# Feed-forward block products summed in the accumulator: one bank grows p1, p6, p7, p4, another p5, p3

## The chip, the core and the metric

The kernel runs on one core of a Trainium2 chip. The metric is the device time of one execution in microseconds (us). The core has five instruction queues that matter here: TensorE (PE, matrix multiply; PEld is its weight load), VectorE (DVE), ScalarE (ACT), GpSimd (POOL) and SyncE (SP, which issues the DMAs). Each queue runs its instructions in the order in which they stand; they wait for each other by semaphores.

## The reference

One inference step of a one-layer encoder. 512 prompt frames and 8 x 16 sample frames make 640 tokens of width 2048. After two kinds of attention and an output projection comes a SwiGLU block with 5632 hidden columns, which takes the larger part of the time and is what the change touches:

```python
def merge_and_ffn(x, oa, ob, norm_grp_a, norm_grp_b, w_out, norm_ffn, w_gate, w_up, w_down):
    o = jnp.concatenate([rmsnorm(oa, norm_grp_a), rmsnorm(ob, norm_grp_b)], axis=-1)
    x = x + o @ w_out
    h = rmsnorm(x, norm_ffn)
    return x + (jax.nn.silu(h @ w_gate) * (h @ w_up)) @ w_down
```

## The kernel before

Everything is float32. A product of two float32 matrices is made of three fast matmuls: each operand is split in a rounded high half (made by ACT, L138) and the rest, the low half (made by DVE, L139), and `mm3` adds high x high, high x low and low x high in PSUM (L147, L148, L149).

In the feed-forward block the products are not taken plainly. Weights and activations are cut in 2 x 2 blocks, and seven products p1 to p7 of sums of blocks give the four result blocks c11, c12, c21, c22 (Winograd's form of Strassen's scheme), instead of eight. The generator `quartet` makes these seven products for one quartet of blocks: it loads the weight blocks b11, b12, b21, b22 by DMA, forms b12-b22 and s6 = b11-(b12-b22) on DVE (L826, L828), b22-s6 and b21-s6 on POOL (L830, L837), and `product` splits one weight operand (list "H" holds six tiles, so three products' halves exist at once) and issues the matmuls of one product: k blocks x 3, with 320 columns. After each product it yields the PSUM bank, and the caller adds that bank where it belongs (L847) or copies it (L886, L960). With u = p1+p6 the results are c11 = p1+p2, c12 = u+p5+p3, c22 = u+p7+p5, c21 = u+p7+p4.

- The loop over w_gate and w_up runs 44 quartets with k = 8: 24 matmuls a product. Activations h stay in SBUF as seven sets of halves (`hs`). Behind each w_gate quartet stand a norm factor, Silu and another factor (L909 to L911), behind each w_up quartet the product with the gate (L915) and the sums for the next stage on POOL (L919 to L922), which four DMAs write to DRAM (act_d).
- w_down runs 32 steps t (`step`), with k = 5 (t below 8 and from 24) or 6, so 15 or 18 matmuls a product. Each of the 8 column groups q is visited four times; its sums x and y stay in SBUF, and u = p1+p6 has a sum of its own over the four visits (tile `us`), which the last visit (t from 24) adds to c21, c22 and c12. Between steps one pair of activations leaves and another is fetched from act_d and split (L857 to L860).
- The last w_up quartet also fetches and splits the five pairs that step 0 needs (`free`, L871), product by product.
- Steps 30 and 31 are cut in an "early" part (p1, p6, p7, p5, p4: the second half of the tokens is finished first) and a "late" part (p2, p3), with the final norm between.

Weight tiles ("W") are six slots in turn: a load waits until the last reader of the slot's former tile is done. PSUM has two pairs of banks (`n.banks()`, named dn) and four single banks (`n.bank()`, named at). Before, a quartet took both pairs: x[:, 0] for p1, x[:, 1] for p5, y[:, 0] for p6, y[:, 1] for p3; p7, p2 and p4 had single banks. The order in each queue is set by the Tile framework's scheduler, not by the order of the source alone.

Of the kernel before, what the change touches and what calls it, by code (L numbers as in the profile page):

```python
# [7 lines left out]
AF = mybir.ActivationFunctionType  # L8
# [5 lines left out]
P = 128  # L14
# [35 lines left out]
class Net:  # L50
# [94 lines left out]
    def mm3(self, out, a, b, first, last):  # L145
        mm = self.nc.tensor.matmul
        mm(out, a[0], b[0], start=first, stop=False)  # L147
        mm(out, a[0], b[1], start=False, stop=False)  # L148
        mm(out, a[1], b[0], start=False, stop=last)  # L149
# [85 lines left out]
def build(nc, tc, io, pools):  # L235
# [557 lines left out]
    def quartet(k, load, lefts, before=None, after=None, part="all"):  # L793

        def product(src, which, bank):
            own = n.get("H"), n.get("H")
            hl = [r(sh(x, k, P)) for x in own]  # L800
            n.split(sh(src, k, P), *hl)
            if before:
                before(which)
            for j in range(k):
                n.mm3(bank, (hl[0][:, j], hl[1][:, j]), lefts[j][which][1], j == 0, j == k - 1)
            n.put("H", *own)
            if after:
                after(which)
            return bank

        def get(i):
            t = n.get("W")
            dma(out=sh(t, k, P), in_=load(i))
            return t

        w = slice(0, k * P)
        sub = ALU.subtract
        if part == "late":
            b21, b22 = get(2), get(3)
            for name, src, which in (("p2", b21, 4), ("p3", b22, 6)):  # L820
                yield name, product(src, which, n.bank()[:, :HT])
                n.put("W", src)
            return
        x, y = n.banks(), n.banks()
        b12, b22, b11 = get(1), get(3), get(0)
        nc.vector.tensor_tensor(b12[:, w], b12[:, w], b22[:, w], sub)  # L826
        s6 = n.get("W")
        nc.vector.tensor_tensor(s6[:, w], b11[:, w], b12[:, w], sub)  # L828
        yield "p1", product(b11, 0, x[:, 0])
        nc.gpsimd.tensor_tensor(b11[:, w], b22[:, w], s6[:, w], sub)  # L830
        yield "p6", product(s6, 1, y[:, 0])
        yield "p7", product(b12, 2, n.bank()[:, :HT])
        n.put("W", b12)
        b21 = get(2)
        if part == "all":
            yield "p2", product(b21, 4, n.bank()[:, :HT])
        nc.gpsimd.tensor_tensor(b21[:, w], b21[:, w], s6[:, w], sub)  # L837
        n.put("W", s6)
        yield "p5", product(b11, 3, x[:, 1])
        n.put("W", b11)  # L840
        yield "p4", product(b21, 5, n.bank()[:, :HT])
        n.put("W", b21)
        if part == "all":
            yield "p3", product(b22, 6, y[:, 1])
        n.put("W", b22)
# [31 lines left out]
    for i in range(NPAIR):  # L877
        for src in ("w_gate", "w_up"):
# [5 lines left out]
            for step, bank in quartet(8, load, hs, (lambda w: next(prep)) if start else None, free if end else None):  # L884
                if step == "p1":
                    nc.scalar.activation(c11, bank, AF.Identity)  # L886
                elif step == "p6":
                    add(c12, c11, bank)
                elif step == "p7":
                    add(c21, c12, bank)  # L890
                elif step == "p5":
                    add(c22, c21, bank)
                    add(c12, c12, bank)
                elif step == "p2":
                    add(c11, c11, bank)
                elif step == "p4":
                    add(c21, c21, bank)
                elif step == "p3":
                    add(c12, c12, bank)
# [37 lines left out]
    def step(t, part="all"):  # L937
        now = active(t)
        nxt = active(t + 1) if t + 1 < STEPS else []
        cnt, q, last = len(now), t % 8, t >= STEPS - 8  # L940
# [6 lines left out]
        if t < 8:  # L947
            x, y = n.get("S"), n.get("S")
            dma(out=x, in_=x2_d[q])
            dma(out=y, in_=x2_d[q + 8])  # L950
            sums.append((x, y, n.get("S") if q % 2 == 0 else sums[-1][2]))
        x, y, u = sums[q]
        c11, c21, c12, c22 = x[:, :HT], x[:, HT:], y[:, :HT], y[:, HT:]
        us = u[:, HT * (q % 2):HT * (q % 2) + HT]
        o = 2 * sum(len(active(i)) for i in range(q, t, 8))
        load = lambda z: io["w_down"][q + 8 * (z % 2), :, o + cnt * (z // 2):o + cnt * (z // 2) + cnt]
        for name, bank in quartet(cnt, load, [lefts[j] for j in now], None, after, part):
            if name == "p1":
                if t < 8:
                    nc.scalar.activation(us, bank, AF.Identity)  # L960
                else:
                    add(us, us, bank)
                add(c11, c11, bank)
            elif name == "p6":
                add(us, us, bank)
                if last:
                    for c in (c21, c22, c12):
                        add(c, c, us)
            elif name == "p7":
                add(c21, c21, bank)  # L970
                add(c22, c22, bank)
            elif name == "p5":
                add(c22, c22, bank)
                add(c12, c12, bank)
            elif name == "p2":
                add(c11, c11, bank)
            elif name == "p4":
                add(c21, c21, bank)
            elif name == "p3":
                add(c12, c12, bank)  # L980
# [147 lines left out]
```

## Time and profile before

| what | value |
|---|---|
| three timed runs, median | 2710.97 us (2708.78 to 2711.12) |
| the profiled execution: time, span | 2706.72 us, 2705.0 us |
| mean granted TensorE clock | 0.986 |
| PE, DVE, ACT, POOL busy | 97%, 71%, 40%, 29% of the span |
| w_gate and w_up | from about 1000 us to about 2095 us |
| w_down, steps 0 to 31 | from about 2095 us to about 2680 us |

The profile is of one execution. Its groups give the mean duration of like instructions, the timeline each instruction with the idle time before it and what ended it, and the table by windows the busy time and the number of instructions of each engine in a stretch. Matmuls overlap their neighbours, so in a stretch without waits the number of matmuls says more than the busy time.

### The profile page before, as it was taken

How to read it: one execution, taken by the hardware profiler on the slowest of the kernel's cores; microseconds unless marked ns; L12 is line 12 of the kernel's file. 1: busy time of each engine (PE TensorE's matmuls, PEld its weight loads, DVE VectorE, ACT ScalarE, POOL GpSimd, SP SyncE). 2: the span in 40 equal slices, each digit the busy share in tenths (PEclk: the TensorE clock that was granted, in tenths of full speed). 3: DMA queues.
4: the chain of work that ended last, by engine and by line, in shares of the span. 5: the costliest groups of instructions: out<-in, count | busy, mean ns of one | idle time of the engine just before them, and what ended most of it. 6: DMA issues, size and time to landing. Idle time of an engine off the chain costs nothing.

```text
span 2705.0 us, 44972 instructions
## 1 busy us (share of the span) xinstructions
PE 2629.3 (97%) x17629; PEld 2568.5 (95%) x17629; DVE 1928.6 (71%) x2956; ACT 1084.0 (40%) x1759; POOL 786.9 (29%) x564
## 2 busy tenths in 40 slices
PE   7999999999999999999999999999999999999986
PEld 7999999999899999999999999999999899999986
DVE  7565565665766777667767666676668888888897
ACT  4333343444633553333333333333334444444443
POOL 3000000000211123343333333433334534444453
PEclk9999999999999999999999999999999899999997
DMA  5222223333556443333333333333335644444344
GB/s 166 85 73 82 89 68 108 109 119 114 183 187 217 147 134 104 104 119 103 105 115 108 108 121 100 119 102 109 113 106 173 214 130 127 132 133 130 107 116 135
DMA packets 154147, 332.23 MB, mean 123 GB/s; under 512 B 18064, under 2 KB 69264, under 8 KB 153936
## 3 DMA queue, kind: packets, MB, share of 16 engines
q1 hardware_dynamic: 153936, 329.38, 38.8%
q8 instruction: 138, 2.26, 0.4%
q14 instruction: 73, 0.60, 0.1%
HBM read 274.38 MB, written 54.20 MB: 121 GB/s over the span
## 4 chain that ended last, share of the span: by engine, by line
PE 84%; DVE 8%; DMA 4%; issue 3%; ACT 2%; SPq 0%; DVEq 0%; POOL 0%; ACTq 0%
PE dn L147 18%; PE dn L149 17%; PE dn L148 17%; PE at L147 9%; PE at L149 9%; PE at L148 9%; DVE W L139 2%; PE at L254 1%; DVE S L847 1%; DMA S<-act_d 1%; DMA W<-w_down 1%; DVE S L139 1%; PE at L155 1%; PE at L154 1%; DVE S L1018 0%
## 5 line engine op out<-in xcount | busy, mean ns | idle before, releaser
L147 PE MATMUL dn<-S,W 128*128 128x320 f32 x3694 | 1165.9, 316 | 15.4 <-DVE S L847 9.6
L149 PE MATMUL dn<-S,W 128*128 128x320 f32 x3694 | 1152.1, 312 | 14.0 <-DVE W L139 13.8
L148 PE MATMUL dn<-S,W 128*128 128x320 f32 x3694 | 1150.3, 311 | 1.1 <-DVE S L139 1.1
L138 ACT ACTIVATE W<-W 128x1024 fp32r<-128x1024 f32 (+2 forms) x632 | 609.3, 965 | 1045.1 <-PE dn L148 518.0
L139 DVE TENSOR_TENSOR W<-W,W 128x1024 fp32r<-128x1024 f32 (+2 forms) x632 | 768.3, 1216 | 126.6 <-ACT W L138 122.3
L147 PEld LDWEIGHTS dn<-S,W 128*128 128x128 f32 x3694 | 700.6, 190 | 33.2 <-issue 16.9
L149 PEld LDWEIGHTS dn<-S,W 128*128 128x128 f32 x3694 | 700.3, 190 | 19.4 <-DVE W L139 18.9
L148 PEld LDWEIGHTS dn<-S,W 128*128 128x128 f32 x3694 | 701.1, 190 | 3.0 <-DVE S L139 1.3
L149 PE MATMUL at<-S,W 128*128 128x320 f32 x1594 | 494.4, 310 | 7.0 <-DVE W L139 6.6
L147 PE MATMUL at<-S,W 128*128 128x320 f32 x1594 | 493.5, 310 | 1.5 <-ACT W L138 1.5
L148 PE MATMUL at<-S,W 128*128 128x320 f32 x1594 | 493.0, 309 | 0.0
L830 POOL TENSOR_TENSOR W<-W,W 128x1024 f32<-128x1024 f32 (+2 forms) x76 | 162.5, 2138 | 588.0 <-DVE W L139 519.0
L149 PEld LDWEIGHTS at<-S,W 128*128 128x128 f32 x1594 | 299.5, 188 | 10.2 <-DVE W L139 10.2
L147 PEld LDWEIGHTS at<-S,W 128*128 128x128 f32 x1594 | 299.9, 188 | 1.7 <-ACT W L138 1.7
L148 PEld LDWEIGHTS at<-S,W 128*128 128x128 f32 x1594 | 299.6, 188 | 0.0
L847 DVE TENSOR_TENSOR S<-S,dn 128x320 f32<-128x320 f32 x358 | 164.2, 482 | 97.6 <-PE dn L149 97.6
L826 DVE TENSOR_TENSOR W<-W,W 128x1024 f32<-128x1024 f32 (+2 forms) x76 | 134.5, 1770 | 103.9 <-DMA W<-w_up 52.4
L837 POOL TENSOR_TENSOR W<-W,W 128x1024 f32<-128x1024 f32 (+2 forms) x76 | 165.5, 2178 | 111.9 <-DVE W L139 106.5
L847 DVE TENSOR_TENSOR S<-S,at 128x320 f32<-128x320 f32 x262 | 123.5, 481 | 70.1 <-PE at L149 70.0
L218 POOL TENSOR_TENSOR S<-S,S 128x640 f32<-128x640 f32 x40 | 75.7, 1893 | 155.5 <-ACT S L217 155.1
L828 DVE TENSOR_TENSOR W<-W,W 128x1024 f32<-128x1024 f32 (+2 forms) x76 | 82.9, 1091 | 30.7 <-DMA W<-w_gate 24.1
L139 DVE TENSOR_TENSOR S<-at,S 128x512 fp32r<-128x512 f32 (+2 forms) x109 | 64.1, 600 | 50.3 <-ACT S L138 49.9
(149 smaller groups left out, 2351.0 us busy)
## 6 DMA issues: line engine op xcount, KB each, us to landing
W<-w_gate SPq DMA_DIRECT2D x88, 512.0 KB
W<-w_up SPq DMA_DIRECT2D x88, 512.0 KB
W<-w_in SPq DMA_DIRECT2D x66, 512.0 KB
W<-w_down SPq DMA_DIRECT2D x64, 384.0 KB
W<-w_down SPq DMA_DIRECT2D x68, 320.0 KB
act_d<-S SPq DMA_DIRECT2D x66, 320.0 KB
half<-act_d SPq DMA_DIRECT2D x81, 160.0 KB
S<-act_d SPq DMA_DIRECT2D x80, 160.0 KB
```

The source lines that it names most:

```text
L138: self.nc.scalar.activation(hi, src, AF.Identity)
L139: self.nc.vector.tensor_tensor(lo, src, f(hi), ALU.subtract)
L147: mm(out, a[0], b[0], start=first, stop=False)
L148: mm(out, a[0], b[1], start=False, stop=False)
L149: mm(out, a[1], b[0], start=False, stop=last)
L154: mm(out, a, b[0], start=first, stop=False)
L218: (eng or nc.gpsimd).tensor_tensor(ssq, ssq, sq, ALU.add)
L826: nc.vector.tensor_tensor(b12[:, w], b12[:, w], b22[:, w], sub)
L828: nc.vector.tensor_tensor(s6[:, w], b11[:, w], b12[:, w], sub)
L830: nc.gpsimd.tensor_tensor(b11[:, w], b22[:, w], s6[:, w], sub)
L837: nc.gpsimd.tensor_tensor(b21[:, w], b21[:, w], s6[:, w], sub)
L847: add = lambda o, a, b: nc.vector.tensor_tensor(o, a, b, ALU.add)
```

## The change

p1, p6, p7 and p4 now go to one bank x of one pair, without clearing it in between (`first=False`; the new argument `more` of `mm3` only lifts the check that a group is closed): after p1 the bank holds p1, after p6 u, after p7 u+p7 and after p4 u+p7+p4. p5 and p3 go to the other bank y of the pair in the same way. Only p2 has a single bank. Each bank is read after each product and before the next product that adds to it. `us`, its tiles and its adds are gone. The order becomes p1, p2, p6, p5, p7, p3, p4; the first quartet ("lean") keeps p1, p6, p7, p2, p5, p4, p3, and the "early" parts run p1, p5, p6, p4, p7. The loads come in the order b11, b21, b12, b22. In w_gate and w_up four of the seven reads are now copies on ACT and three are adds on DVE (one copy and seven adds before); in w_down there are seven adds on DVE (9 and a copy for t below 8, 10 up to t = 23, 13 from t = 24).

```diff
-        mm(out, a[0], b[0], start=first, stop=False)
+        mm(out, a[0], b[0], start=first, stop=False, skip_group_check=more)
...
+        pair_of = n.banks()
+        x, y = pair_of[:, 0], pair_of[:, 1]
+        b11 = get(0)
+        def sums():
+            b12, b22, s6 = get(1), get(3), n.get("W")
+            minus(b12, b12, b22)
+            minus(s6, b11, b12)
+            return b12, b22, s6
...
+        b21 = get(2)
+        yield "p1", product(b11, 0, x)
...
+        yield "p2", product(b21, 4, alone())
+        b12, b22, s6 = sums()
+        yield "p6", product(s6, 1, x, False)
+        minus(b11, b22, s6, nc.gpsimd)
+        yield "p5", product(b11, 3, y)
+        n.put("W", b11)
+        minus(b21, b21, s6, nc.gpsimd)
+        n.put("W", s6)
+        yield "p7", product(b12, 2, x, False)
+        n.put("W", b12)
+        yield "p3", product(b22, 6, y, False)
+        n.put("W", b22)
+        yield "p4", product(b21, 5, x, False)
+        n.put("W", b21)
...
+            into = {"p1": c11, "p2": c11, "p6": c12, "p3": c12, "p5": c22, "p7": c22, "p4": c21}
+            copied = ("p1", "p6", "p7" if start else "p5", "p4")
...
+                c = into[step]
+                if step in copied:
+                    nc.scalar.activation(c, bank, AF.Identity)
+                else:
+                    add(c, c, bank)
...
-            if name == "p1":
-                if t < 8:
-                    nc.scalar.activation(us, bank, AF.Identity)
-                else:
-                    add(us, us, bank)
-                add(c11, c11, bank)
-            elif name == "p6":
-                add(us, us, bank)
-                if last:
-                    for c in (c21, c22, c12):
-                        add(c, c, us)
...
+            for c in into[name]:
+                add(c, c, bank)
```

DVE in step 26 of w_down, before. S_3196 holds c11 and c21, S_3197 c12 and c22, S_3198 the sum u; L139 rows make low halves, L826 is the next step's b12-b22. The rows run from the reads of p1 (bank dn_26498) to the reads of p7 (at_26554) and p2 (at_26583):

```order
2680 L847 TENSOR_TENSOR S_3198_21663<-S_3198_21663,dn_26498 128x320
2681 L847 TENSOR_TENSOR S_3196_21659<-S_3196_21659,dn_26498 128x320
2682 L139 TENSOR_TENSOR W_4047_26585<-W_4044_26581,W_4046_26584 128x640
2683 L826 TENSOR_TENSOR W_4067_26695<-W_4067_26695,W_4068_26697 128x640
2684 L847 TENSOR_TENSOR S_3198_21663<-S_3198_21663,dn_26499 128x320
2685 L139 TENSOR_TENSOR W_4051_26611<-W_4033_26504,W_4050_26610 128x640
2686 L847 TENSOR_TENSOR S_3196_21659<-S_3196_21659,S_3198_21663 128x320
2687 L847 TENSOR_TENSOR S_3197_21660<-S_3197_21660,S_3198_21663 128x320 x2
2688 L847 TENSOR_TENSOR S_3196_21659<-S_3196_21659,at_26554 128x320
2689 L847 TENSOR_TENSOR S_3197_21660<-S_3197_21660,at_26554 128x320
2690 L139 TENSOR_TENSOR W_4056_26638<-W_4044_26581,W_4055_26637 128x640
2691 L847 TENSOR_TENSOR S_3196_21659<-S_3196_21659,at_26583 128x320
```

The same step on DVE now (S_3057 is c11 and c21, S_3058 is c12 and c22, both banks are called dn_26156), from the read of p1 to that of p5 at row 2466; L898 is a fetched activation's low half, L818 are b12-b22 and s6 of the next step:

```order
2457 L885 TENSOR_TENSOR S_3057_21470<-S_3057_21470,dn_26156 128x320
2458 L139 TENSOR_TENSOR W_3831_26236<-W_3816_26157,W_3830_26235 128x640
2459 L885 TENSOR_TENSOR S_3057_21470<-S_3057_21470,at_26181 128x320
2460 L139 TENSOR_TENSOR W_3835_26262<-W_3823_26202,W_3834_26261 128x640
2461 L898 TENSOR_TENSOR S_3853_26366<-S_3854_26367,S_3853_26366 128x320
2462 L885 TENSOR_TENSOR S_3058_21471<-S_3058_21471,dn_26156 128x320
2463 L139 TENSOR_TENSOR W_3839_26287<-W_3824_26204,W_3838_26286 128x640
2464 L818 TENSOR_TENSOR W_3860_26398<-W_3860_26398,W_3861_26400 128x640
2465 L818 TENSOR_TENSOR W_3862_26402<-W_3849_26343,W_3860_26398 128x640
2466 L885 TENSOR_TENSOR S_3058_21471<-S_3058_21471,dn_26156 128x320
2467 L139 TENSOR_TENSOR W_3843_26312<-W_3817_26159,W_3842_26311 128x640
```

The three adds from u are gone, each product has one read, and both subtractions of the next step's weights stand together between the low half of p3 (row 2463) and the read of p5 (row 2466).

ACT in a w_gate quartet before: the high halves (L138) of p7, p2, p5, p4 and p3, and the one copy, of p1 (row 1055):

```order
1053 L138 ACTIVATE W_2930_19827<-W_2921_19758 128x1024
1054 L138 ACTIVATE W_2934_19859<-W_2932_19856 128x1024
1055 L886 ACTIVATE S_2917_19754<-dn_19756 128x320
1056 L138 ACTIVATE W_2936_19889<-W_2923_19762 128x1024
1057 L138 ACTIVATE W_2939_19920<-W_2932_19856 128x1024
1058 L138 ACTIVATE W_2941_19949<-W_2922_19760 128x1024
```

And now, from the high half of p5 (row 940) to the copy of p4 (951). The copies of p1, p6 and p5 are rows 942, 945 and 947; between them stand the high halves of p7, p3 and p4 and of the next quartet's p1, p2 and p6, and a Silu (L941):

```order
940 L138 ACTIVATE W_2381_15371<-W_2369_15271 128x1024
941 L941 ACTIVATE S_2343_15042<-S_2343_15042 128x640
942 L928 ACTIVATE S_2366_15268<-dn_15270 128x320
943 L138 ACTIVATE W_2383_15401<-W_2376_15334 128x1024
944 L138 ACTIVATE W_2385_15430<-W_2377_15336 128x1024
945 L928 ACTIVATE S_2367_15269<-dn_15270 128x320
946 L138 ACTIVATE W_2387_15459<-W_2370_15273 128x1024
947 L928 ACTIVATE S_2367_15269<-dn_15270 128x320
948 L138 ACTIVATE W_2394_15505<-W_2392_15501 128x1024
949 L138 ACTIVATE W_2397_15535<-W_2393_15503 128x1024
950 L138 ACTIVATE W_2402_15571<-W_2401_15568 128x1024
951 L928 ACTIVATE S_2366_15268<-dn_15270 128x320
```

A copy stands behind the high half that is made when its own product ends, and it is what p6, p7 and p3 now wait for before they may add to their bank.

More of the change, by code (lines that the diff above doesn't have):

```diff
@@ L804, in product @@
             for j in range(k):
-                n.mm3(bank, (hl[0][:, j], hl[1][:, j]), lefts[j][which][1], j == 0, j == k - 1)
+                n.mm3(bank, (hl[0][:, j], hl[1][:, j]), lefts[j][which][1], first and j == 0, j == k - 1, not first)
             n.put("H", *own)
@@ L820, in quartet @@
             for name, src, which in (("p2", b21, 4), ("p3", b22, 6)):
-                yield name, product(src, which, n.bank()[:, :HT])
+                yield name, product(src, which, alone())
                 n.put("W", src)
             return
[L824 to L828, printed above, removed]
@@ new lines, in quartet @@
+        b21 = get(2)
+        yield "p1", product(b11, 0, x)
+        if part == "early":
+            b12, b22, s6 = sums()
+            minus(b11, b22, s6, nc.gpsimd)
+            yield "p5", product(b11, 3, y)
+            n.put("W", b11, b22)
+            minus(b21, b21, s6, nc.gpsimd)
+            yield "p6", product(s6, 1, x, False)
+            n.put("W", s6)
+            yield "p4", product(b21, 5, alone())
+            n.put("W", b21)
+            yield "p7", product(b12, 2, x, False)
+            n.put("W", b12)
+            return
```

82 lines of the change are left out of this document (29 added, 53 removed).

## The prediction

> **What bounds the kernel now.** I read the busy times first, then PE by windows, then the chain of waits and the timeline where PE falls short.
>
> ```profile
> PE 2629.3 (97%) x17629; PEld 2568.5 (95%) x17629; DVE 1928.6 (71%) x2956; ACT 1084.0 (40%) x1759; POOL 786.9 (29%) x564
> 1300.00:1700.00 400.00, 400.00 (x2730) 400.00 (x2729) 277.08 (x294) 138.22 (x146) 151.04 (x83) 1.00 0.34 109
> 2080.00:2100.00 20.00, 16.49 (x99) 15.06 (x98) 20.00 (x28) 14.16 (x31) 12.45 (x11) 0.93 0.78 266
> 2100.00:2120.00 20.00, 16.13 (x92) 15.41 (x92) 14.83 (x22) 6.20 (x13) 10.98 (x10) 0.81 0.72 234
> 2120.00:2140.00 20.00, 18.47 (x112) 17.94 (x113) 18.71 (x26) 9.83 (x18) 9.06 (x8) 0.91 0.71 226
> 2520.00:2540.00 20.00, 20.00 (x139) 20.00 (x138) 15.17 (x24) 7.28 (x11) 6.94 (x5) 1.00 0.38 102
> 2540.00:2560.00 20.00, 18.92 (x126) 18.21 (x125) 17.57 (x30) 9.58 (x16) 7.49 (x5) 1.00 0.39 113
> 2560.00:2580.00 20.00, 17.89 (x117) 17.09 (x117) 18.87 (x27) 9.61 (x17) 10.44 (x7) 1.00 0.40 113
> 2580.00:2600.00 20.00, 16.30 (x110) 15.80 (x109) 18.67 (x27) 10.11 (x18) 12.58 (x8) 1.00 0.46 131
> 2600.00:2620.00 20.00, 18.58 (x123) 17.82 (x122) 19.89 (x30) 8.11 (x13) 8.95 (x6) 1.00 0.38 106
> 2620.00:2640.00 20.00, 18.17 (x121) 17.34 (x120) 18.78 (x26) 10.04 (x18) 12.44 (x8) 1.00 0.34 96
> 2640.00:2660.00 20.00, 15.73 (x80) 14.40 (x79) 16.56 (x21) 9.44 (x18) 12.51 (x9) 0.76 0.40 124
> ```
>
> The columns after the stretch and its length are PE, PEld, DVE, ACT and POOL (busy us and instructions), the granted clock, and the DMA share. In w_gate and w_up PE is never idle: 400 us / 2730 = 0.1465 us a matmul, so a product of 24 lasts 3.52 us, one of 18 (k = 6) 2.64, one of 15 (k = 5) 2.20. The change issues the same matmuls, so there nothing can be won. A full slice of 20 us holds 139 matmuls (2520 to 2540). What is missing elsewhere: from 2080 to 2140, the passage from w_up to w_down, 417 - 303 = 114, or 16.7 us; from 2540 to 2640, steps 24 to 29, 695 - 597 = 98, or 14.4 us; from 2640 to 2660, the early parts, 59, or 8.6 us. These 40 us are all that a lighter DVE could give. In the last of the five slices from 2540 DVE was busy 18.78 of 20, in all five 93.8 of 100.
>
> ```profile
> 2103.36 0.61 PE L147 MATMUL dn<-S,W 128*128 128x320 f32 x1 [3.83 <-DVE S L847]
> 2119.29 0.39 PE L147 MATMUL dn<-S,W 128*128 128x320 f32 x1 [0.29 <-DVE S L847]
> 2121.33 0.64 PE L149 MATMUL dn<-S,W 128*128 128x320 f32 x1 [1.52 <-DVE W L139]
> 2127.02 0.31 PE L147 MATMUL at<-S,W 128*128 128x320 f32 x1
> 2587.16 0.39 PE L147 MATMUL dn<-S,W 128*128 128x320 f32 x1 [2.28 <-DVE S L847]
> ```
>
> PE waits there for DVE: for a low half (L139) or for an add that frees a dn bank (L847). After the wait of 3.83 us a matmul takes 0.61 us instead of 0.31. The product from 2119.29 to 2127.02 took 7.73 us: 2.20 of work, 1.52 of waiting, 4.0 of slowed matmuls.
>
> **The change part by part.** First the reads of PSUM.
>
> ```profile
> L847 DVE TENSOR_TENSOR S<-S,dn 128x320 f32<-128x320 f32 x33 | 14.8, 477 | 0.0
> L847 DVE TENSOR_TENSOR S<-S,S 128x320 f32<-128x320 f32 x18 | 11.8, 708 | 0.0
> L139 DVE TENSOR_TENSOR W<-W,W 128x640 fp32r<-128x640 f32 x40 | 46.5, 1162 | 1.5 <-ACT W L138 1.3
> L826 DVE TENSOR_TENSOR W<-W,W 128x640 f32<-128x640 f32 x5 | 7.4, 1481 | 4.0 <-DMA W<-w_down 3.9
> L828 DVE TENSOR_TENSOR W<-W,W 128x640 f32<-128x640 f32 x6 | 4.9, 818 | 0.0
> ...
> L886 ACT ACTIVATE S<-dn 128x320 f32<-128x320 f32 x31 | 13.0, 420 | 0.0
> L138 ACT ACTIVATE W<-W 128x1024 fp32r<-128x1024 f32 x213 | 226.4, 1063 | 465.4 <-PE at L148 216.9 <-PE dn L148 209.7 <-issue 32.7
> ```
>
> The first five groups are DVE's from 2540 to 2640, the last two ACT's from 1300 to 2050. A late step loses its three adds from u (0.708 each) and three of ten reads of PSUM (0.477): 3.56 us. Over the 5.5 steps of that stretch (100 us at 18.2, below) this is 19.6 of DVE's 93.8 us, and 74 remain for the 86 us that PE needs. So PE bounds these steps again: -14.4 at most. Steps 8 to 23 lose three reads, steps 0 to 7 two and a copy, at a time when PE hardly waits: nothing. A quartet of w_gate or w_up loses four adds on DVE, 1.9 us, and gains three copies on ACT, 1.3 us of 24.6, where ACT is busy 138 of 400: nothing either, if the copies come in time.
>
> **The new waits.** Each product that adds to a bank waits until the bank's last sum is read, and one product lies between. In w_gate and w_up the copy of p1 stands behind the high half of p5, which waits for p1's end to get its tile: 1.06 + 0.42 = 1.5 us after p1, and p6 starts at 3.5. This is covered by p2, with 2 us to spare; p6, p5 and p4 are alike. The copy of p6 in a w_gate quartet writes the tile whose former content a DMA still carries to act_d. That DMA is now the last of four, behind the copy of p4, a multiplication and four POOL sums.
>
> ```profile
> 1699.55 1.80 POOL L919 TENSOR_TENSOR S<-S,S 128x320 f32<-128x320 f32 x1 [1.21 <-DVE S L915]
> 1701.42 0.88 POOL L921 TENSOR_TENSOR S<-S,S 128x320 f32<-128x320 f32 x1
> ...
> 1652.09 0.37 SPq L925 DMA_DIRECT2D act_d<-S  x1
> 1656.05 0.49 DVE L847 TENSOR_TENSOR S<-S,dn 128x320 f32<-128x320 f32 x1 [0.99 <-PE dn L149]
> ```
>
> In the trace the write issued at 1652.09 did not hold up the add at 1656.05: at most 4 us. After p4 I count 1.5 (copy), 2.1 (low half, multiplication), 5.4 (sums at 1.8, 1.8, 0.9, 0.9) and 0.7 (two issues): issue at 9.7, end by 12.5 to 13.7; p7 must start at 14.1. Covered by 0.4 to 1.6 us: I take 0, with +0.8 x 22 = +17 if the write is slower.
>
> In w_down the tight one is the read of p5. It stands behind both subtractions of the next step's weights, whose b22 can be loaded only when the low half of p7 has freed its slot.
>
> ```profile
> 2422.66 0.33 SPq L813 DMA_DIRECT2D W<-w_down  x1
> 2425.97 0.96 DVE L826 TENSOR_TENSOR W<-W,W 128x768 f32<-128x768 f32 x1 [0.64 <-DMA W<-w_down]
> ...
> L139 DVE TENSOR_TENSOR W<-W,W 128x768 fp32r<-128x768 f32 x77 | 92.7, 1204 | 3.8 <-ACT W L138 3.8
> L138 ACT ACTIVATE W<-W 128x768 fp32r<-128x768 f32 x76 | 64.5, 849 | 104.6 <-PE dn L148 43.2 <-PE at L148 37.2 <-issue 11.8
> L826 DVE TENSOR_TENSOR W<-W,W 128x768 f32<-128x768 f32 x10 | 19.0, 1899 | 7.5 <-DMA W<-w_down 7.5
> L828 DVE TENSOR_TENSOR W<-W,W 128x768 f32<-128x768 f32 x11 | 10.5, 952 | 0.4 <-DMA W<-w_down 0.2
> ...
> 2606.33 2.95 DMA W<-w_down
> ```
>
> From the end of p2, with k = 6: high and low half of p7 0.85 + 1.20, the load 3.31, two subtractions 0.95 to 1.90 and 0.95, the add 0.48: 7.7 to 8.7 us. p3 wants its bank after p6, p5 and p7, at 7.92: 0 to 0.8 us late. With k = 5: 0.72 + 1.16 + 2.95 (row 2606.33) + 0.82 to 1.48 + 0.82 + 0.48 = 6.95 to 7.6 against 6.60: 0.35 to 1.0 late (0.72 is 640 columns at the 849 ns for 768, with a little fixed cost). Over steps 1 to 23 (seven with k = 5, sixteen with 6) that is 2.5 to 20 us; uncontended halves are nearer, since the contended mean comes from overlap with POOL's subtractions, which now stand elsewhere: +5. For steps 24 to 29 it gives back about 3 of the 14.4: -11, ends -14 and -4.
>
> **The other places.** In the passage from w_up to w_down DVE loses 1.9 us of its 20 busy out of 20, but the copies of p1, p6 and p5 now stand on ACT between fetched activations that wait for their DMA.
>
> ```profile
> 2069.35 0.74 ACT L910 ACTIVATE S<-S 128x640 f32<-128x640 f32 x1
> 2075.81 1.20 ACT L859 ACTIVATE S<-S 128x320 fp32r<-128x320 f32 x3 [2.06 <-DMA S<-act_d]
> ```
>
> ACT's extra work behind p1 is a high half, a Silu, three fetches and the copy, 1.06 + 0.74 + 1.2 + 0.42 = 3.4 against 3.52: the cover is nearly gone. I take -3, ends -10 and +6. The early parts lose four adds each and PE may keep its clock there: -4, ends -10 and +4. The first quartet keeps p1, p6, p7 in a row in one bank, without a product between: two reads in the open, each a high half and a copy or a copy alone, 1.5 + 0.6, and some queueing: +3, ends +1 and +5.
>
> The sum: -11 - 4 - 3 + 3 + 5 + 0 = -10. The profiled execution took 2706.7 us, 1.7 above its span, so 2697; the median of the runs lies 4.3 above it: 2701 us.
>
> **The rivals.** (A) The forecast: 2701, own range 2690 to 2708.
>
> (B) On the other side: the read of p5 is late in most steps, at the upper end. One mechanism: the load of b22, released by p7's low half. It decides once it lands over 2T + 0.5 us behind p2, T being a product. +20 instead of +5, and 6 instead of 3 in the late steps: 2701 + 18 = 2719. For it speaks that L826 already waited 7.5 us for loads in ten steps; against it that PE had no wait there.
>
> (C) The late steps aren't bound by DVE's work but by a loop of loads.
>
> ```profile
> by line: issue 21.7%; DVE S L847 21.4%; DVE W L139 20.0%; DMA W<-w_down 16.7%; DMA S<-act_d 7.0%; DVE W L828 2.7%; DVE S L860 2.6%; ACT W L138 2.5%; ACT S L217 1.4%; ACT S L1015 1.0%; PE at L149 0.8%; PE dn L148 0.5%; PE dn L147 0.5%; PE dn
> 2540.46 1.28 DVE S L847 x3
> ...
> 2631.44 1.27 DVE S L847 x3
> ```
>
> Between the first and the last of six such triples lie 91 us, 18.2 a step against 15.4 of matmuls. The chain there is DVE for half, but loads for 17%. If they hold the step, the -11 goes: 2712.
>
> (D) The copy of p6 waits for act_d: +17, 2718.
>
> (E) With DVE lighter, the stretches at 2080 and 2640 lose their stalls and slow clock as well: -14.4 + 3 - 10 - 8.6 + 3 + 3 = -24, 2687.
>
> (F) Many short waits for banks pull the clock down: +4.0 in each of 31 steps by the product at 2119.29, about 2820. Against it: from 2540 to 2640 the clock stayed at 1.00 through waits up to 2.28 us. The Trainium skill has this as a rule (TensorE: Matmul & The Clock Gate, "A second HAM failure mode: psum-queue depth-cycling"): short PE idles between groups of matmuls that cycle through PSUM can make the clock gate oscillate. The rows from 2540 do not bear it out, the slow matmul at 2121.33 does.
>
> **How the numbers follow.** Chances: A 0.48, B 0.17, C 0.15, D 0.08, E 0.09, F 0.03. What a measurement can tell from no change is about 0.2%, 5.4 us. Faster: A 0.44, E 0.09, C and B 0.04: 0.57. Same: A 0.04, C 0.10, B and D 0.05: 0.19. Slower: 0.24. The range 2685 to 2723 leaves out F, the lower half of E and the ends of B and D.
>
> **What would show it.** The late steps: 139 matmuls a slice from 2540 on and DVE under 90%. B: PE L147 on dn waiting for DVE's add in each step of w_down, and DVE's subtraction waiting for w_down ahead of it. D: ACT's copy waiting for a DMA to act_d in every second quartet. The start: two PE waits of 0.5 to 2 us on ACT's copy near 1005. I am wrong if the matmuls from 1300 to 2050 show gaps at all, or if the passage near 2100 costs more than 23 us.

## The result, and the profile after

The changed kernel took 3043.85 us (median of 4 runs, 3032.33 to 3047.26) against 2709.88 us before: 1.1229 times the time, 95% interval 1.1213 to 1.1245. The forecast was 2701 us. The page's busy times of the changed kernel, and below them its table by windows, over the 400 us of w_gate and w_up that were shown of before and over w_down (steps 1 to 24):

```profile
PE 2714.9 (89%) x17629; PEld 2598.0 (85%) x17629; DVE 1749.7 (57%) x2672; ACT 1128.2 (37%) x1883; POOL 751.5 (25%) x564
```

```profile
1300.00:1700.00 400.00, 349.16 (x2287) 336.68 (x2285) 196.29 (x192) 130.59 (x165) 118.96 (x68) 1.00 0.29 94
2344.70:2560.00 215.30, 180.45 (x1114) 172.14 (x1113) 122.65 (x179) 73.00 (x115) 60.54 (x46) 0.95 0.39 112
2560.00:2860.00 300.00, 257.18 (x1611) 246.58 (x1610) 173.18 (x231) 102.27 (x153) 87.53 (x62) 0.96 0.36 100
```

Every engine is less busy than before, as a share, so no engine has become the bound: somebody waits. In w_gate and w_up, where PE had 2730 matmuls in 400 us, it now has 2287, and a quartet takes 24.6 x 2730 / 2287 = 29.4 us. Whom PE waits for stands in the table of waits from 1300 to 2050 (us in total, times, longest):

```profile
PE dn L147 <- ACT S L928: 76.3, 52, 1.9
PE dn L147 <- DVE S L885: 17.5, 25, 0.7
```

and in the timeline of one quartet (the first matmuls of five products; then ACT's and DVE's rows that PE waits for):

```profile
1504.27 0.31 PE L147 MATMUL at<-S,W 128*128 128x320 f32 x1
1507.79 0.31 PE L147 MATMUL dn<-S,W 128*128 128x320 f32 x1
1512.80 0.42 PE L147 MATMUL dn<-S,W 128*128 128x320 f32 x1 [1.32 <-ACT S L928]
1517.95 0.42 PE L147 MATMUL dn<-S,W 128*128 128x320 f32 x1 [1.37 <-ACT S L928]
1522.39 0.41 PE L147 MATMUL dn<-S,W 128*128 128x320 f32 x1 [0.65 <-DVE S L885]
...
1511.37 1.06 ACT L138 ACTIVATE W<-W 128x1024 fp32r<-128x1024 f32 x1 [2.46 <-PE dn L148]
1512.33 0.42 ACT L928 ACTIVATE S<-dn 128x320 f32<-128x320 f32 x1
...
1521.85 0.49 DVE L885 TENSOR_TENSOR S<-S,dn 128x320 f32<-128x320 f32 x1 [3.02 <-PE dn L149]
```

p2, in the single bank (at), starts at 1504.27 and p6 at 1507.79, both without a wait. The three waits are those of p5, p7 and p3. p5 (1512.80) starts when the copy of p6 (1512.33 to 1512.75) is done, although p5 writes bank y and the copy reads bank x; p7 (1517.95) starts after the copy of p5; p3 (1522.39) after the add that reads p7 (1521.85 to 1522.34). Each of these three waits for the read of the product just before it, in the other bank. The prediction had one product between a read and the wait for it; there is none.

Where the time went, by the moments at which 6660 matmuls are recorded from the start and 3560 are left to the end (the same matmuls in each kernel; all columns but the median are of the profiled execution):

| kernel | median us | start to matmul 6660 | w_gate, w_up, step 0 | the last 3560 (w_down from step 1 on) |
|---|---|---|---|---|
| before | 2710 | 1031 | 1104 | 570 |
| changed | 3044 | 1030 | 1314 | 701 |
| y in a tile of its own | 2777 | 1034 | 1152 | 586 |
| and Silu behind the copy of p1 | 2750 | 1036 | 1121 | 589 |
| and u written early | 2732 | 1030 | 1109 | 589 |
| and squares on DVE | 2722 | 1033 | 1107 | 578 |
| and reads first in steps 8 to 23 | 2711 | 1033 | 1107 | 568 |

The rows below the second are the experiments, each with the edits of the rows above it.

### The profile page after: what moved, and what is told of

Its sections match the earlier page's. It is cut to its first block, busy times and chain, and to the rows that moved or that the text cites. A ratio compares the mean times of both kernels' runs of the same rounds, so it can differ in the third digit from the quotient of the medians.

```text
span 3045.5 us, 44909 instructions
## 1 busy us (share of the span) xinstructions
PE 2714.9 (89%) x17629; PEld 2598.0 (85%) x17629; DVE 1749.7 (57%) x2672; ACT 1128.2 (37%) x1883; POOL 751.5 (25%) x564
## 5 line engine op out<-in xcount | busy, mean ns | idle before, releaser
L147 PE MATMUL dn<-S,W 128*128 128x320 f32 x4740 | 1530.6, 323 | 285.6 <-DVE S L885 134.8
L148 PE MATMUL dn<-S,W 128*128 128x320 f32 x4740 | 1487.0, 314 | 2.6 <-DVE S L143 1.6
L149 PE MATMUL dn<-S,W 128*128 128x320 f32 x4740 | 1474.6, 314 | 4.7 <-DVE W L139 4.6
L147 PEld LDWEIGHTS dn<-S,W 128*128 128x128 f32 x4740 | 908.3, 192 | 366.8 <-ACT S L928 154.2
L138 ACT ACTIVATE W<-W 128x1024 fp32r<-128x1024 f32 (+2 forms) x632 | 608.1, 963 | 1338.2 <-PE dn L148 1097.3
L139 DVE TENSOR_TENSOR W<-W,W 128x1024 fp32r<-128x1024 f32 (+2 forms) x632 | 742.6, 1175 | 361.2 <-ACT W L138 352.5
L148 PEld LDWEIGHTS dn<-S,W 128*128 128x128 f32 x4740 | 910.1, 192 | 5.1 <-DVE S L143 1.8
L149 PEld LDWEIGHTS dn<-S,W 128*128 128x128 f32 x4740 | 906.3, 192 | 6.1 <-DVE W L139 5.7
L818 POOL TENSOR_TENSOR W<-W,W 128x1024 f32<-128x1024 f32 (+2 forms) x152 | 326.6, 2149 | 922.9 <-DVE W L139 838.3
L885 DVE TENSOR_TENSOR S<-S,dn 128x320 f32<-128x320 f32 x280 | 135.6, 485 | 382.4 <-PE dn L149 381.9
L818 DVE TENSOR_TENSOR W<-W,W 128x1024 f32<-128x1024 f32 (+2 forms) x152 | 166.8, 1097 | 112.1 <-DMA W<-w_up 59.4
L898 POOL TENSOR_TENSOR S<-S,S 128x320 fp32r<-128x320 f32 x102 | 108.1, 1062 | 284.7 <-ACT S L897 276.4
L147 PE MATMUL at<-S,W 128*128 128x320 f32 x548 | 169.6, 309 | 1.5 <-ACT W L138 1.5
L149 PE MATMUL at<-S,W 128*128 128x320 f32 x548 | 169.4, 309 | 0.0
L148 PE MATMUL at<-S,W 128*128 128x320 f32 x548 | 169.3, 309 | 0.0
L897 ACT ACTIVATE S<-S 128x320 fp32r<-128x320 f32 x189 | 84.2, 464 | 113.5 <-PE dn L149 56.8
L218 POOL TENSOR_TENSOR S<-S,S 128x640 f32<-128x640 f32 x40 | 74.1, 1851 | 161.3 <-ACT S L217 160.7
L147 PEld LDWEIGHTS at<-S,W 128*128 128x128 f32 x548 | 103.0, 188 | 1.8 <-ACT W L138 1.8
L942 POOL TENSOR_TENSOR S<-S,S 128x640 f32<-128x640 f32 x44 | 79.2, 1801 | 98.5 <-ACT S L941 98.5
L149 PEld LDWEIGHTS at<-S,W 128*128 128x128 f32 x548 | 103.0, 188 | 0.0
L148 PEld LDWEIGHTS at<-S,W 128*128 128x128 f32 x548 | 102.9, 188 | 0.0
L139 DVE TENSOR_TENSOR S<-at,S 128x512 fp32r<-128x512 f32 (+2 forms) x109 | 64.0, 599 | 50.4 <-ACT S L138 49.9
```

What stands on the lines that cost most here:

```text
L138: self.nc.scalar.activation(hi, src, AF.Identity)
L139: self.nc.vector.tensor_tensor(lo, src, f(hi), ALU.subtract)
L147: mm(out, a[0], b[0], start=first, stop=False, skip_group_check=more)
L148: mm(out, a[0], b[1], start=False, stop=False, skip_group_check=more)
L149: mm(out, a[1], b[0], start=False, stop=last, skip_group_check=more)
L218: (eng or nc.gpsimd).tensor_tensor(ssq, ssq, sq, ALU.add)
```

## The experiments

**One tile or two.** Theory T: the program waits for the tile (a pair of banks is one tile), not for the bank. The first run only puts y in a tile of its own:

```diff
-        pair_of = n.banks()
-        x, y = pair_of[:, 0], pair_of[:, 1]
+        x, y = n.banks()[:, 0], alone()
```

> The changed kernel, but bank y (p5, p3) is a single bank of its own tile instead of the other half of the pair that holds x. Order and number of matmuls, adds and copies are left alone. Theory T (the framework waits for the tile, not for the bank: a product that writes y waits until the read of x just before it is done, and the other way round): the four waits of 0.6 to 1.5 us in each quartet of w_gate and w_up go (44 x 4.4 = 194 us), and most of the 145 us in w_down; what remains is the blind forecast with its terms, 2701 us, 2690 to 2723. Rival R (a bank that is read and grown again is slow in itself, or ACT's copies come too late for their own bank): the waits stay and the time is 3000 to 3050.

Measured: 2776.99 us (1.0248 of before, 1.0230 to 1.0267). 267 of the 334 us are gone. The two profiled executions lie 273 us apart, 158 of it before the last 3560 matmuls and 115 in them. T holds, R falls; but 2777 isn't 2701.

The second run takes `x, y = n.banks()[:, 0], n.banks()[:, 0]`:

> The changed kernel with x and y in two different pairs, one bank of each used. The pool has two pairs, so each quartet takes the same two again. Theory T: inside a quartet no product waits for a read just before it, but p1 of the next quartet writes the pair that p4's read has to leave, so one wait a quartet remains: about 1.5 us (high half 1.06, copy 0.42) x 43 = 65 in w_gate and w_up and 0.7 to 1 x 30 = 25 in w_down: some 90 us above the kernel with y in a single bank, about 2790 (2760 to 2820). Rival R: 3000 to 3050 as in the changed kernel.

Measured: 2775.77 us (1.0222 to 1.0257), the same as with the single bank. The gain came again, the wait at p1 that I expected did not: PE's waits for ACT's copies from 1300 to 2050 came to 20.8 us, against 20.3 in the run before. In the trace of this run p1 follows p4 without an idle, and the copy of p4 (1526.41) only starts while p1 already runs, so p1 can't have been given the pair of p4, as I had assumed. Which pair it got I did not follow up.

The third run changes before: `product(s6, 1, x[:, 1])` and `product(b11, 3, y[:, 0])`, so that p1 and p6 share a pair.

> The kernel before, with nothing grown and nothing moved, only the pairs dealt out otherwise: p1 and p6 (neighbours in its order) get the two banks of one pair, p5 and p3 those of the other. Theory T: p6 now waits for the read of p1, 1.5 us (high half 1.06, copy 0.42) x 44 = 66 us in w_gate and w_up, and 1 to 2.5 us (one or two adds behind DVE's other work) x 32 = 32 to 80 in w_down: 2810 to 2855. Rival R: no bank is grown and the copy has the time of a whole product as before, so 2710, no change.

Measured: 2722.45 us, 1.0050 of before (1.0035 to 1.0065): a loss, but 14 us instead of 100. In PE's order p7 is now cut in two: in w_gate and w_up ten of its 24 matmuls stand between p1 and p6. The planner (the Tile framework's scheduler) had seen the wait of about 1.5 us and filled it with 10 x 0.1465 = 1.5 us of other work. A number from such a run is a price after the planner's answer, not the price of the wait; that a shared pair would make neighbours wait in the kernel before, too, rests here on this order, not on the time. The same sign stood in the changed kernel's order before any run: the next p1 cut in 2 and 6 around p4.

**What was left in w_gate and w_up.** With y apart PE still waits once or twice in each pair of quartets. Two such places in the timeline of that kernel (POOL, DVE, ACT and PE; then ACT and PE):

```profile
1501.48 3.40 POOL L818 TENSOR_TENSOR W<-W,W 128x1024 f32<-128x1024 f32 x1
1502.53 3.03 DVE L939 TENSOR_TENSOR S<-S,S 128x640 f32<-128x640 f32 x1
1505.59 0.74 ACT L940 ACTIVATE S<-S 128x640 f32<-128x640 f32 x1 [4.60 <-DVE S L939]
1506.23 0.42 ACT L927 ACTIVATE S<-dn 128x320 f32<-128x320 f32 x1
1506.70 0.42 PE L147 MATMUL dn<-S,W 128*128 128x320 f32 x1 [1.19 <-ACT S L927]
...
1486.92 0.44 ACT L927 ACTIVATE S<-dn 128x320 f32<-128x320 f32 x1 [2.39 <-DMA act_d<-S]
1487.41 0.41 PE L147 MATMUL dn<-S,W 128*128 128x320 f32 x1 [0.31 <-ACT S L927]
```

The copy of p1 stands on ACT behind a Silu of the quartet before, the Silu waits for DVE's factor, and that multiplication takes 3.03 us beside a POOL subtraction of 3.40. The second case is rival D: the copy of p6 waits for the write to act_d. The next runs move a write ahead of POOL's four sums; order that Silu behind the copy of p1; give p3 a third bank in w_down; and do all three. Their main lines:

```diff
+                send(y[1], slice(4, 6))
...
+                        factor(gate[0], done)
...
-        yield "p3", product(b22, 6, y, False)
+        yield "p3", product(b22, 6, *((y, False) if k == 8 else (alone(),)))
```

> The kernel with y in a tile of its own (2777 us), and the DMA that carries the tile of c12 and c22 to act_d issued before POOL's four sums instead of last; it only reads that tile, so nothing else changes. In the kernel of 2777 us ACT's copy of p6 in each w_gate quartet waits 2.1 to 2.5 us for that DMA, and p7 starts 0.2 to 0.45 us late (0.5 with the slow first matmul). Theory D (the rival of the prediction): these waits go, 22 x 0.5 = 11 us, 2766 (2760 to 2770). Rival Q (only the queue order of the Silu counts): the ACT wait is beside the path, no change, 2774 to 2780.

> The kernel with y in a tile of its own (2777 us), and the Silu of the tile c11, c21 of each w_gate quartet forced behind the copy of the next quartet's p1 in ACT's queue (no wait of its own, only the order). In the kernel of 2777 us this Silu waits 4.6 us for DVE's multiplication (3.0 us beside POOL, 0.8 alone), and the copy of p1 stands behind it; p6 waits 1.19 us and its first matmul is slow, 1.5 in all, once in each pair of quartets. Theory Q: 22 x 1.5 = 33 us go, 2744 (2738 to 2752). Rival D: the copy comes free but the copy of p6 then waits longer for its act_d write, since all is earlier and the write is not; 2760 to 2777. Rival: the low halves behind the multiplication on DVE become the wait; no change.

> The kernel with y in a tile of its own (2777 us), and in w_down p3 in a third bank: c12 gets p5 and p3 by two adds, one add more on DVE in each step, but p3 no longer waits until p5 is read. Theory B (p5's read, behind the subtractions of the next step's weights, costs the 16.5 us by which w_down there is longer than before): w_down gets 10 to 15 us shorter, 2763 to 2768. Rival W (the reads of p6 and p7 stand behind the same subtractions and p7 and p4 wait for them instead): 2772 to 2780.

> The three edits together: y in a tile of its own, c12's write first, Silu behind the copy of p1, p3 in a third bank in w_down. If the three costs add up: 2777 - 11 - 33 - 12 = 2721 (2712 to 2730), still not under the kernel before, since w_gate and w_up can't go below what they took there. If one wait hides another: 2735 to 2760.

Measured: 2777.27, 2749.73, 2787.42 and 2757.95 us. The Silu was worth 27 us by the medians (33 expected), 31 in the column of w_gate and w_up. The write was worth nothing, and ACT's waits for act_d stayed as they were (25.2 us from 1300 to 2050, 24.7 with y apart): I had moved the wrong one. By the turns of the tiles in their slots, the copy of p6 writes the slot of the gate's tile u (s3, s1) of the pair before, not that of c12 and c22. A third bank for p3 cost 10 us: in w_down up to 2700 us PE's waits for DVE's adds at p3 are gone (12.4 us with y apart), but those at the products of bank x went from 9.9 to 26.5 us. So the wait moved, as rival W had it; that the extra add on DVE made it longer is likely, but not shown. The three together are about the sum of these. The write of u, issued behind the two sums that fill it:

```diff
                 tt(s3, c21, c11, ALU.subtract)
+                dma(out=act_d[2:4, :, i].rearrange("w p c -> p w c"), in_=halves(u))
                 tt(s2, s1, c11, ALU.subtract)
```

> The kernel with the Silu behind the copy of p1 (2750 us), and the write of tile u (s3 and s1) to act_d issued as soon as the two sums that fill it are made, behind two POOL sums instead of four. The names of the tiles say that this is the tile which the copy of p6 in the next w_gate quartet writes; the write moved in the earlier run was that of another tile. Theory D in its mended form: ACT's waits of 2.1 to 2.4 us for act_d go, and with them up to 22 x 0.5 = 11 us: 2739 to 2745. Rival (these waits never reach PE now): 2746 to 2753, although the ACT waits go.

Measured: 2731.88 us, 18 less by the medians (11 at most expected); the copies of p6 no longer wait at all. The four runs of the kernel it is compared with spread from 2738 to 2755 us, so the 27 and the 18 are each open by some 10 us; in the column of w_gate and w_up this edit is worth 12. The window from 1300 to 1700 with y apart:

```profile
1300.00:1700.00 400.00, 387.22 (x2605) 381.93 (x2605) 271.89 (x217) 145.58 (x188) 145.34 (x77) 1.00 0.33 107
```

with the Silu moved:

```profile
1300.00:1700.00 400.00, 398.43 (x2706) 396.58 (x2705) 280.65 (x225) 150.84 (x193) 151.03 (x80) 1.00 0.34 109
```

and with u written early:

```profile
1300.00:1700.00 400.00, 400.00 (x2730) 400.00 (x2729) 261.46 (x228) 152.56 (x194) 144.88 (x82) 1.00 0.34 110
```

2730 again, the count of before. All but 5 of the 210 us that the column of w_gate and w_up had lost are accounted for by three waits: the pair, the Silu ahead of a copy, the write of u.

**w_down.** 19 us more than before were left there. The term of the prediction that should have gained, the late steps, I tested on the kernel before, by leaving out DVE work in steps 24 to 29 (the other three places alike):

```diff
+        light = STEPS - 8 <= t < STEPS - 2
...
-                if last:
+                if last and not light:
                     for c in (c21, c22, c12):
                         add(c, c, us)
```

> The kernel before, with the DVE work that the change saves left out of steps 24 to 29 of w_down and nothing else changed: the three adds from u, and one of the two reads of p1, p7 and p5 (what is left out is part of the sums, so these results are incomplete). 3.56 us of DVE less in each of six steps. Term of the prediction (DVE bounds these steps): 11 to 14 us shorter, about 2697. Rival C (a loop of loads bounds them): 0 to -3 us, 2706 to 2709.

Measured: 0.9970 of before (0.9958 to 0.9982), 8 us less, which is under the 11 to 14 expected and over rival C's 3. The 652 matmuls that are 800 to 150 from the end took 111 us instead of 120; they are most of steps 24 to 29 and the first part of the early parts. Steps 24 to 29 alone went from 106.1 to 99.1 us, where their 630 matmuls need 92.3 at 0.1465. So the term is real: DVE's work cost these steps 7 of the 14 us that they lose; what holds the other 7 this run does not show. And in the kernel of 2732 us the same 652 matmuls take 121 us, although DVE has become light. Before:

```profile
2544.60:2664.50 119.90, 104.90 (x652) 99.59 (x651) 109.49 (x154) 55.04 (x94) 64.40 (x41) 0.94 0.40 115
```

The 2732 kernel:

```profile
2565.90:2687.10 121.20, 100.85 (x652) 97.38 (x651) 89.41 (x115) 53.24 (x93) 62.07 (x41) 0.97 0.38 113
```

DVE went from 109.5 to 89.4 us and the stretch didn't follow. In steps 8 to 23 the loss was what the prediction had described, PE waiting for the read of p5 and then once more. In the timeline of the 2732 kernel, and in its table of waits over w_down:

```profile
2373.92 0.39 PE L147 MATMUL at<-S,W 128*128 128x320 f32 x1 [0.95 <-DVE S L884]
2377.14 0.39 PE L147 MATMUL dn<-S,W 128*128 128x320 f32 x1 [0.35 <-DVE S L884]
```

```profile
DVE W L818 <- DMA W<-w_down: 44.6, 24, 3.4
```

Four runs on that: the subtractions on POOL (`minus` with POOL for k below 8, on the kernel of 2777 us, and once on the kernel of 2732 us), the loads in another order (`ahead = (get(1), get(3))` before b21), and `minus(b12, b12, b21)` in place of b22.

> The kernel with y in a tile of its own (2777 us), and in w_down both subtractions b12-b22 and s6 on POOL, so that no read of a bank stands behind them on DVE. Theory W (reads of p6 and p5 stand on DVE behind subtractions that wait for b22's load, and p7, p3 and p4 wait for those reads): the 16.5 us by which w_down is longer than before go, and the late steps may win what the forecast said: 2750 to 2762. Rival C (the loads themselves hold the steps, whichever engine subtracts): 2772 to 2780. Rival P (POOL's longer subtractions slow DVE beside them): 2770 to 2790.

> Own tile for y, Silu behind the copy of p1, u written early, subtractions of w_down on POOL, together. If the costs add up (2777 - 30 - 8 - 16): 2723; under the kernel before (2709) only if the late steps win their 11 us too. If POOL's subtractions cost more than they free: 2740 to 2760.

> The kernel with y in a tile of its own, Silu behind the copy of p1 and u written early (2732 us), and in w_down the weight blocks loaded in the order b11, b12, b22, b21 instead of b11, b21, b12, b22. The last load of the four waits for the slot that p7's low half frees; now that is b21, which p2 needs, and no longer b22, which DVE's first subtraction needs. Theory W (w_down's excess of 18.7 us over the kernel before is reads of banks that stand on DVE behind a subtraction waiting for b22): 10 to 18 us go, 2714 to 2722, and if the late steps win what the light steps won (9 us), 2708. Rival C (the loads as such bound the steps): 2728 to 2736. Rival: p2 now waits for b21, no gain or a loss of up to 10 us.

> The kernel of 2732 us again, and in w_down the first subtraction takes b21, which is loaded earlier, in place of b22 (b12 - b21 instead of b12 - b22, so the results of w_down are not those of the reference; number, size and engine of the instructions are the same). No load moves; only the wait of DVE for b22 is gone. Theory W: as for the other load order, 2712 to 2722. If the other order of loads gains and this one doesn't, it was the loads and not DVE's wait; if this one gains and the other doesn't, p2 pays for it there.

Measured: 2788.92, 2744.45, 2729.44 and 2731.47 us. POOL's subtractions cost 12 us: the late stretch went from 121 to 128. The two runs that made the wait for b22 shorter gained 5 us in the profiled w_down and nothing clear in the medians. DVE still waited 43.5 and 37.3 us for loads in w_down (44.6 above): the planner, which now expected the block earlier, had moved the subtraction ahead of another read. PE's waits for DVE's adds at bank y, p3's, fell from 11.4 to 3.2 and 2.9 us, but those at bank x rose from 16.5 to 21.1 and 17.4. So I fixed its place:

```diff
+            first = minus(b12, b12, b22)
+            if k < 8 and reads:
+                n.tc.add_manual_dep(first.ins, reads[-1].ins.name, after_it, reason="queue order")
```

> The kernel of 2732 us, and in w_down the first subtraction of the next step's weights (b12 - b22) forced behind the read of p3 in DVE's queue, an order only and no wait of its own; the planner had put it ahead of the reads of p6 or p5, and in the two runs before it had moved it ahead again when the load was made earlier, so that the wait came back at p7 instead of at p3. Theory W (a read stands on DVE behind a subtraction that waits for a load; p3, p7 and p4 wait for that read): PE's waits for DVE's adds in steps 1 to 23 go, and with them 10 to 16 us of w_down's 18.7, and in the late steps 5 to 9 more: 2708 to 2722. Rival C (loads bound the steps): 2728 to 2736, with the waits turned into waits of PE for the halves of s6 (p6).

Measured: 2732.89 us, no change. Steps 8 to 23, however, gained: from 2240 to 2480 there were 1639 matmuls before, 1564 in the 2732 kernel, 1610 here, which is 46 x 0.1465 = 6.7 us. The rows, in this order:

```profile
2240.00:2480.00 240.00, 240.00 (x1639) 240.00 (x1637) 202.39 (x275) 102.28 (x154) 97.70 (x62) 1.00 0.47 130
```

```profile
2240.00:2480.00 240.00, 233.90 (x1564) 230.60 (x1563) 188.13 (x227) 98.36 (x151) 99.33 (x63) 0.99 0.42 123
```

```profile
2240.00:2480.00 240.00, 238.50 (x1610) 237.57 (x1610) 198.85 (x233) 101.05 (x154) 97.30 (x63) 0.99 0.43 128
```

Steps 24 to 29 gave 6 of it back and steps 1 to 7 another 4 (the late stretch took 128 instead of 121 us). What holds the late steps is in the chain of waits of the 2732 kernel, and in its timeline:

```profile
2633.16 2.17 POOL S L218
2635.39 2.05 POOL S L218
2637.46 2.30 DMA S<-act_d
...
2649.67 2.16 POOL S L218
2651.90 2.06 POOL S L218
2653.97 2.20 DMA S<-act_d
```

```profile
2619.14 0.83 ACT L896 ACTIVATE S<-S 128x320 fp32r<-128x320 f32 x2 [6.12 <-DMA S<-act_d]
2621.08 0.61 PE L147 MATMUL dn<-S,W 128*128 128x320 f32 x1 [4.29 <-ACT S L896]
```

L218 adds the squares of a finished step to the sum for the norm, on POOL. As soon as its second add ends, a fetch from act_d starts: it takes the S slot that the squares held. Behind the fetch wait ACT, the products, and DVE's queue. So the last two runs put these adds on DVE, which has room now, and (second run) kept the fixed place of the subtraction for k = 6 alone:

```diff
-                n.add_square(ssq, sums[t % 8][i], t == STEPS - 8 and i == 0, "S")
+                n.add_square(ssq, sums[t % 8][i], t == STEPS - 8 and i == 0, "S", nc.vector)
...
-            if k < 8 and reads:
+            if k == 6 and reads:
```

> The kernel of 2732 us, and the sum of squares behind each of the steps 24 to 29 (two adds of 640 columns a step) on DVE instead of POOL. In the 2732 kernel DVE is busy 89 of 121 us in the late stretch, against 109 of 120 in the kernel before, and the stretch is no shorter; the chain there runs over POOL's two squares of 2.1 us and straight from the second to a fetch from act_d, which takes the place that the squares held. Theory S (POOL's squares hold the fetch and so the late steps; the prediction's relief of DVE was real, and the next thing was late): the stretch gets 5 to 11 us shorter, 2721 to 2727. Rival L (the loads of weights and activations bound it whatever POOL does): 2730 to 2734.

> The same, and in the steps with k = 6 (8 to 23) the first subtraction of the step's weights behind the read of p3, as in the run that won 7 us in those steps and lost as much in the late ones. If both add up to the 2732 kernel: 2732 - 7 - 8 = 2717 (2712 to 2724), near to the kernel before but not under it. If the late stretch undoes the gain again: 2728 to 2734.

Measured: 2721.72 us (1.0051 of before, 1.0038 to 1.0064) and 2711.01 us (1.0010, 1.0001 to 1.0019), 10 and 21 us less than 2732 (the 21 more than the 15 expected). The late stretch took 110 us in both, against 120 before and 121; S holds, L falls. ACT's waits for act_d in that stretch fell from 28.4 us (longest 6.1) to 14.5 (longest 2.5). The run takes the adds off POOL altogether, so the slot and POOL's own queue, in which its subtractions stand beside the squares, are not told apart. The same window as above, with the squares on DVE, has 732 matmuls instead of 652, with more on DVE and a third less on POOL:

```profile
2565.90:2687.10 121.20, 110.40 (x732) 106.50 (x732) 98.56 (x139) 60.48 (x103) 40.69 (x30) 1.00 0.40 115
```

With five edits the changed kernel takes the time of the kernel before. None of the versions beats it.

Where w_down's time went, by steps (the same matmuls of each kernel, counted back from the end, us of the profiled execution; the first row is the number of matmuls x 0.1465, that is, no wait at all):

| kernel | steps 1 to 7 | 8 to 23 | 24 to 29 | early parts |
|---|---|---|---|---|
| no wait | 107.7 | 295.3 | 92.3 | 22.0 |
| before | 116.7 | 295.7 | 106.1 | 32.9 |
| before, with DVE work left out of steps 24 to 29 | 115.5 | 295.7 | 99.1 | 30.9 |
| 2732 | 119.5 | 307.1 | 111.3 | 29.0 |
| 2732, subtraction behind the reads | 123.5 | 299.8 | 117.1 | 29.9 |
| 2732, squares on DVE | 119.1 | 307.7 | 102.8 | 26.3 |
| 2732, squares on DVE, and subtraction behind the reads for k = 6 (2711) | 117.8 | 300.4 | 102.8 | 26.3 |

## Why the prediction was wrong, step by step

- **"Each product that adds to a bank waits until the bank's last sum is read, and one product lies between."** This sentence failed, and with it 267 us. The wait is for the tile, the pair, so the read that counts is that of the product just before, and its whole length (a high half of 1.06 and a copy of 0.42) lies open. The "2 us to spare" were those of the bank. Before, neighbours in time never shared a pair, so its trace had no such wait; the rule had to be asked for, not assumed. The range had no case for it, and rival F, the only one far up, was another mechanism.
- **w_gate and w_up at 0, rival D at +17.** D was real: 12 us in the profile and 18 by the medians, near the price I had given; what I had wrong was the write that was waited for. The 27 us of the Silu had no term: I asked what ACT had to do between p1 and its copy in the passage to w_down, and not in each pair of quartets, and I took DVE's factor at its time alone, not at 3.0 us beside POOL.
- **The read of p5 behind the subtractions, +5, ends 2.5 and 20; rival B.** The mechanism was right. In the 2732 kernel steps 1 to 23 take 14.2 us more than before, in the upper half; with the subtraction behind the reads, the 11.4 us that steps 8 to 23 lose there became 4.1 (4.7 in the 2711 kernel). I took the value near the uncontended end, and the other was nearer.
- **Late steps, -11.** "So PE bounds these steps again" failed too: with DVE's work left out, the kernel before gained 7 us in steps 24 to 29, half of what PE waits there. In the 2732 kernel they took 5.2 us more than before instead of 11 less, and 3.3 less once POOL's squares were moved. That chain, the squares and the fetch behind them, was missing from the sum. Rival C named loads, and the price of C (no gain) is near what happened in the changed kernel's order.
- **Early parts, -4.** With y apart, and in the 2732 kernel, they take 3.8 and 3.9 us less than before: right, within what one profile tells, and for the reason given, since the granted clock, 0.76 from 2640 to 2660 before, is 1.00 in the early parts of the 2732 kernel.
- **The first quartet, +3.** Two waits were forecast near 1005, of 0.5 to 2 us; the changed kernel's PE rows have them, the first a little longer:

```profile
1003.36 0.64 PE L147 MATMUL dn<-S,W 128*128 128x320 f32 x1 [2.27 <-ACT S L928]
1010.05 0.42 PE L147 MATMUL dn<-S,W 128*128 128x320 f32 x1 [0.59 <-ACT S L928]
```

  What they cost in the end is below the spread of the first column above, 1030 to 1036 us.
- **The passage, -3.** The 140 matmuls from 3700 to 3560 before the end take 28.0 us in the 2732 kernel and 25.4 before, so +2.6: on the other side of zero, inside the ends. (In the last kernel of the table they took 24.6.)
- **F, the clock.** From 1300 to 1700 the granted clock stayed at 1.00 through three waits in each quartet; in w_down, with waits up to 2.8 us, it was 0.95 and 0.96 in the windows shown first, against 1.00 from 2240 to 2480 before. The Trainium skill's rule (TensorE: Matmul & The Clock Gate, "A second HAM failure mode: psum-queue depth-cycling") thus agrees with w_down; in w_gate and w_up the clock fell to half only three times from 1100 to 2000 us, for 3.4 us each. What such a fall costs stands in the trace: two windows of 3 us without an idle, a little behind a wait, hold 13 matmuls at half clock and 22 at full.

```profile
2380.40:2383.40 3.00, 3.00 (x13) 3.00 (x12) 0.50 (x1) 0.00 (x0) 0.00 (x0) 0.50 0.41 101
2385.00:2388.00 3.00, 3.00 (x22) 2.89 (x21) 1.60 (x4) 0.77 (x3) 1.71 (x1) 1.00 0.22 60
```

  Added up over the last 3560 matmuls, starts spaced wider than 0.1465 us while the clock was at half cost 26 us in the changed kernel and 5 with y apart. So about 21 of the 115 us that the shared pair cost in w_down were clock, and the rest waits: F's mechanism was real there, behind the waits, at a sixth of its price.

The statement that I would be wrong "if the matmuls from 1300 to 2050 show gaps at all" was the one that told at once where to look.

## What to carry to other kernels

Before costing a wait for a buffer, find out what the program tracks: here two halves of one PSUM tile were one thing, and alternating between them hid nothing. A product cut in two in PE's order was, both times here, the planner filling a wait that it expected. A lighter engine gains only up to the next chain, so look for that chain before counting the gain. Put a copy that frees a bank ahead of anything in its queue that may wait.

## What the hardware showed

DVE's 640-column multiplication took 0.81 us in the changed kernel, alone:

```profile
1504.61 0.81 DVE L940 TENSOR_TENSOR S<-S,S 128x640 f32<-128x640 f32 x1
```

With y apart it took 3.03 us beside POOL's subtraction of 1024 columns, which itself took 3.40 us instead of the 2.41 us that it takes in the same kernel at 1520.71. DVE, busy 272 of 400 us there, so held up PE by the moment at which two engines met, and not by the amount of its work. Growing a bank that is read in between cost nothing by itself: with all waits gone the matmul pace from 1300 to 1700 was that of before, 2730 in 400 us.
